# VectorE alone drains the units made ahead; the first negated copies come later in ScalarE's order; a fifth seven-product pair in layer 0's key and query units

## The chip, the cores and the metric

The kernel runs on one core of one Trainium2 chip. The metric is the device time of one launch in microseconds (us), with all weights read from HBM. A run is the median of several executions; one execution is recorded by the hardware profiler, and the views quoted below are of that one.

## The reference

Two layers of a hybrid decoder trunk on x of 256 rows by 2048 columns, all float32. The part that matters here is matrix products of 256 rows with weights that are read once:

```python
def hybrid_layer(x, attn_norm, w_in, ...):
    h = rms_norm(x, attn_norm)
    proj = jnp.einsum('bsd,de->bse', h, w_in)          # 2048 x 6160
    g_q, g_k, g_v, g_gate, g_lr, s_q, s_k, s_v = jnp.split(proj, COL_SPLITS, axis=-1)
    o_gla = gla_chunked(...)                           # gated linear attention, 8 heads
    o_sb = stick_breaking_attention(sq, sk, s_v)       # 8 heads
    mixed = jnp.concatenate([o_gla, o_sb], axis=-1)
    x = x + jnp.einsum('bse,ed->bsd', mixed, w_o)      # 2048 x 2048
    hm = rms_norm(x, mlp_norm)
    up = jnp.square(jax.nn.relu(jnp.einsum('bsd,df->bsf', hm, w_up)))   # 2048 x 8192
    return x + jnp.einsum('bsf,fd->bsd', up, w_down)   # 8192 x 2048

def reference(x, ...):
    for l in range(DEPTH):                             # DEPTH = 2
        x = hybrid_layer(x, ...)
    return x
```

## The kernel before

**Products.** A float32 product is made of three TensorE products in the rounded type fp32r: high part of the activation by `whi`, high by `wlo`, low by `whi` (`product`, L1231, L1234, L1235; the narrower projections of the attention stage do the same in L630 to L632). Each raw weight tile (1 MB, loaded by SP in L1023) is therefore made twice: ScalarE (ACT) rounds it to `whi` (L1098), then VectorE (DVE) makes `wlo` = raw - `whi` (L1102).

**Units and pairs.** Work goes in units of 1024 output columns by 2048 weight rows, eight pairs of 256 rows, numbered 0 to 7, in an order of steps given by a table. The kinds are g (gate), o (output projection, two units), up and down (16 units a layer), and iv, ik, iq: values, keys and queries made ahead for the next layer (for layer 0 they are the first big units of the program, in the text the first stage; for layer 1 they end layer 0's stage). A plain pair takes 24 products in two steps of 12 (banks 2 and 4, then 3 and 8). A seven-product pair takes 21 in four steps of 6, 6, 6 and 3 (banks 2 and 3, 5 and 7, 1 and 6, 4): it works like Winograd's scheme, and for it VectorE makes sums of weight tiles (`ts`, and two sums into the raw tile, L876) and both engines make other forms of the activation (L471, L488, L492). The tables EACH, FEWER, LATER, O0, O1 and those in OWN hold the order of steps, the seven-product pairs, and the pairs whose weights come by another way: for these GpSimd's queue (POOL) loads the rounded tile `chi` (L1059, function `high`), ScalarE writes `dlo` = -`chi` (L1063, `negated`), and a second DMA adds the weights into `dlo` (L1066). EACH is the order of all three units of the first stage; in layer 0, iv goes by FEWER, ik and iq by LATER.

**What sets the order.** TensorE, SP and POOL work in the order written. For ScalarE and VectorE a planner (`Plan`, `add(engine, cost, function, dependencies...)`) sorts the instructions by due times at build time; the engines then run strictly in that order. `held_tile` (L1054) is a tiny ScalarE write that gives the first three `chi` tiles a place; it is added with no dependency.

**Drains.** The eight accumulators m1 to m8 (bank 1 to 8) of a unit hold seven-product and plain sums and are put together in `up_tail`, which serves up units and the three kinds made ahead (`into` is False for these, and only their code changes). VectorE combines two tiles at a time (`combine`, L876 in the trace). In the kernel before, ScalarE copies bank 1 (L1366), VectorE forms w = b6 - b1, y10 = b5 + w, then w += b7 in place; banks 2 and 3 are added from the bank; banks 4 and 8 are copied by ScalarE first (L1391), and the second read of bank 5 waits for the copy of bank 8. After the last unit of a stage the banks are given back, and the first accumulator of the attention stage (`acc`, L630) lies on bank 5.

**Opening.** Before the first unit, TensorE makes a projection into `acc` (L630 to L632), whose two halves ScalarE copies out in L922 (`values`).

Of the kernel before, what the change touches and what calls it, by code (L numbers as in the profile page):

```python
# [11 lines left out]
F32R = mybir.dt.float32r  # L12
# [11 lines left out]
FEWER = [0, 0, 1, 2, 7, 4, 1, 1, 1, 6, 7, 6, 6, 6, 2, 3, 3, 3, 3, 5, 4, 5], (1, 3, 6), (2, 4)  # L24
# [3 lines left out]
O0 = [4, 5, 7, 4, 6, 6, 0, 0, 0, 7, 1, 0, 1, 1, 1, 5, 2, 2, 2, 2, 3, 3], (0, 1, 2), (5, 7)  # L28
O1 = [4, 6, 4, 1, 1, 2, 1, 5, 1, 2, 0, 0, 2, 2, 0, 5, 0, 3, 6, 3, 7, 7], (0, 1, 2), (5, 6)
SEEDED = (("down", 0), ("down", 1), ("o", 1))  # L30
SPARE = ("sxh",)
OWN = {
    ("up", 0): ([2, 5, 5, 5, 5, 1, 1, 1, 1, 2, 0, 0, 0, 3, 4, 0, 3, 3, 3, 6, 4, 6, 6, 6, 7, 7], (0, 1, 3, 5, 6), (2, 4)),
    ("up", 0, 0): ([0, 0, 3, 4, 3, 3, 1, 3, 4, 1, 1, 1, 5, 5, 2, 5, 5, 6, 6, 2, 6, 6, 7, 7], FAST, (2, 4)),
    ("up", 1): ([7, 7, 5, 5, 4, 5, 5, 1, 1, 1, 2, 3, 1, 3, 3, 3, 4, 6, 6, 6, 6, 0, 2, 0], FAST, (2, 4)),
    ("down", 0): ([0, 0, 1, 1, 1, 3, 4, 1, 3, 5, 3, 3, 4, 5, 5, 5, 2, 6, 6, 6, 6, 7, 7, 2], FAST, (2, 4)),
    ("down", 1): ([7, 7, 3, 3, 4, 3, 3, 5, 5, 5, 4, 5, 1, 1, 1, 1, 0, 0, 2, 0, 0, 6, 6, 6, 6, 2], (0, 1, 3, 5, 6), (2, 4)),
}
CAST, AHEAD_BY = 3, 1
FIRST_RAWS = 6  # L40
# [134 lines left out]
def trunk_kernel(  # L175
# [275 lines left out]
    def forms(op, i, t, tag):  # L451
# [21 lines left out]
        def high():  # L473
            if e:
                if both:
                    if tag in SPARE:
                        op.x[i] = act_tile(F32R, (P, 4, 2, P))
                    else:
                        op.x[i] = tmp(tag + "k", [P, 4, 2, P], F32R, bufs=1)
                elif keep:  # L480
                    op.x[i] = act_tile(F32R, (P, 4, 2, P))
                else:
                    op.x[i] = tmp(tag, [P, 3, 2, P], F32R, bufs=len(FAST))
# [375 lines left out]
    def ordered(l, units, hT, rst, ug, gates_t, mixed=None, ons=None):  # L859
# [182 lines left out]
        def rounded(u, j, s):  # L1042
# [314 lines left out]
        def up_tail(u):  # L1357
# [6 lines left out]
            def copy():  # L1364
                box[0], box[1] = act_tile(F32, (P, NT, 512)), act_tile(F32, (P, NT, 512))
                nc.scalar.activation(box[0][:, 0, :], banks[1], AF.Copy)  # L1366

            def new_dw():
# [12 lines left out]
            if not into:  # L1381
# [2 lines left out]
            def half(h, p):  # L1384
                box["r", h] = []
                for tt, m in enumerate(((2, 4), (3, 8))[h]):
                    before = p[m]
                    if tt:
                        free[m] = before = [add(
                            "ACT", A1,  # L1390
                            lambda m=m, h=h: nc.scalar.activation(  # L1391
# [7 lines left out]
                    users = box.setdefault("users", []) if tt else []  # L1399
                    a = vector(  # L1400
                        y(h, tt), y(h, tt), (lambda: box["w"]) if tt else bk(m), before,
                        box["s"][2 * h + tt], users, op=ALU.subtract if m == 4 else ALU.add,
                    )
                    a.give = len(users)
                    users.append(a)
                    if not tt:
                        free[m] = [a]

                    def relu(tt=tt):
# [556 lines left out]
```

## Time and profile before

| | us |
|---|---|
| median of 3 runs | 2145.78 |
| the runs | 2145.78, 2146.07, 2139.18 |
| profiled execution | 2145.65 |
| its span | 2144.0 |
| granted TensorE clock, mean of full | 0.996 |
| TensorE busy | 2117.9 |
| VectorE busy | 1936.9 |
| ScalarE busy | 1509.6 |
| GpSimd busy | 279.1 |

Times in views count from the start of the span. A timeline row reads: start, duration, engine, line, operation, output<-inputs, shape, count, and in brackets how long the engine had been idle before and what released it. In a row that stands for several instructions the duration is their sum, or for DMA issues the stretch over which they were issued. A row of a queue (SPq) is the issue of a transfer, not its landing. A matmul's duration covers its way through the array, so the pace is read from start to start.

### The profile page before, as it was taken

What the parts mean: (1) busy time and instruction counts of PE and PEld (TensorE: products, weight loads), DVE (VectorE), ACT (ScalarE), POOL (GpSimd) and SP (SyncE); (2) the same over time, 40 slices, a digit from 0 to 9 for tenths busy, and PEclk for the clock granted to TensorE, in tenths of its full rate; (3) what the DMA queues carried; (4) which work ended last, traced back from release to release, by engine and by line L of the source; (5) the groups of instructions that cost most, each with busy time, mean ns of one, the idle gap of its engine ahead of it and who ended that gap; (6) DMA issues with size and microseconds to landing.
All of it is one profiled execution on the core that took longest, in us unless ns stands there. A gap on an engine that the chain in (4) does not pass through costs nothing.

```text
span 2144.0 us, 28336 instructions
## 1 busy us (share of the span) xinstructions
PE 2117.9 (99%) x10040; PEld 1762.7 (82%) x10040; DVE 1936.9 (90%) x2658; ACT 1509.6 (70%) x2044; POOL 279.1 (13%) x394
## 2 busy tenths in 40 slices
PE   8999999999999999999999999999999999999998
PEld 6878888888888888888888888888888888888887
DVE  5887868999999999999998786699999999999998
ACT  6666667777677777668776575677776776786775
POOL 0110001111111111111111000011111111111110
PEclk9999999999999999999999999999999999999999
DMA  8765348788988988987988553678889888889886
GB/s 304 215 192 184 124 136 251 223 251 244 260 258 240 273 255 231 275 261 227 260 252 260 158 173 118 212 220 243 255 253 254 253 259 249 250 256 255 250 246 197
DMA packets 160691, 497.16 MB, mean 232 GB/s; under 512 B 10682, under 2 KB 19458, under 8 KB 160548
## 3 DMA queue, kind: packets, MB, share of 16 engines
q1 hardware_dynamic: 100900, 319.16, 41.3%
q0 software_dynamic: 59648, 176.18, 37.0%
q8 instruction: 79, 1.29, 0.2%
q14 instruction: 64, 0.52, 0.1%
HBM read 493.20 MB, written 2.10 MB: 231 GB/s over the span
## 4 chain that ended last, share of the span: by engine, by line
PE 91%; DVE 3%; ACT 3%; DMA 2%; issue 1%; POOL 0%; ACTq 0%; DVEq 0%
PE acc L630 3%; PE acc L632 3%; PE acc L631 3%; DMA raw<-in_w_in_dram 1%; DVE wlo L1102 1%; ACT whi L611 0%; DMA raw<-in_w_o_dram 0%; ACT whi L1098 0%; DMA chi<-in_w_in_dram 0%; PE ps L1903 0%; DVE wlo L613 0%; PE ps L1896 0%; DVE act L876 0%; PE ps L741 0%; PE ps L1853 0%
## 5 line engine op out<-in xcount | busy, mean ns | idle before, releaser
L1102 DVE TENSOR_TENSOR wlo<-raw,whi 128x1024 fp32r<-128x1024 f32 (+1 forms) x697 | 749.7, 1081 | 75.3 <-ACT whi L1098 41.2
L1098 ACT ACTIVATE whi<-raw 128x1024 fp32r<-128x1024 f32 (+1 forms) x697 | 648.9, 947 | 212.6 <-DVE raw L876 77.8
L1063 ACT ACTIVATE dlo<-chi 128x1024 fp32r<-128x1024 f32 x168 | 177.7, 1058 | 102.1 <-DMA chi<-in_w_in_dram 8.8
L1098 ACT ACTIVATE whi<-ts 128x1024 fp32r<-128x1024 f32 x177 | 187.3, 1058 | 70.0 <-DVE ts L876 33.9
L876 DVE TENSOR_TENSOR ts<-raw 128x1024 f32<-128x1024 f32 x177 | 215.5, 1218 | 11.3 <-DMA raw<-in_w_in_dram 8.6
L1102 DVE TENSOR_TENSOR wlo<-ts,whi 128x1024 fp32r<-128x1024 f32 x177 | 215.3, 1216 | 1.8 <-ACT whi L1098 1.7
L630 PE MATMUL acc<-whi,act 128*128 128x512 f32 (+2 forms) x384 | 142.4, 371 | 4.2 <-DVE act L876 4.2
L611 ACT ACTIVATE whi<-raw 128x1024 fp32r<-128x1024 f32 (+2 forms) x98 | 88.6, 908 | 69.7 <-PE acc L632 66.5
L632 PE MATMUL acc<-whi,act 128*128 128x512 f32 (+2 forms) x384 | 137.7, 359 | 0.0
L631 PE MATMUL acc<-wlo,act 128*128 128x512 f32 (+2 forms) x384 | 137.5, 358 | 0.0
L613 DVE TENSOR_TENSOR wlo<-raw,whi 128x1024 fp32r<-128x1024 f32 (+2 forms) x98 | 100.6, 1031 | 34.8 <-ACT whi L611 34.6
L876 DVE TENSOR_TENSOR raw<-raw 128x512 f32<-128x512 f32 x177 | 121.1, 684 | 1.8
L876 DVE TENSOR_TENSOR raw<-ts,raw 128x512 f32<-128x512 f32 x177 | 120.7, 682 | 0.1
L1059 POOL DMA_DIRECT2D chi<-in_w_up_dram x64 | 38.1, 595 | 515.0 <-PE m__2883_13592 L1235 34.8
L1059 POOL DMA_DIRECT2D chi<-in_w_down_dram x64 | 41.6, 650 | 424.6 <-PE m__914_4357 L1235 22.1
L630 PEld LDWEIGHTS acc<-whi,act 128*128 128x128 f32 x384 | 73.4, 191 | 17.1 <-DVE act L876 5.0
L1066 POOL DMA_DIRECT2D dlo<-in_w_down_dram x64 | 65.3, 1020 | 151.9 <-ACT dlo L1063 123.5
L632 PEld LDWEIGHTS acc<-whi,act 128*128 128x128 f32 x384 | 73.2, 191 | 10.4
L631 PEld LDWEIGHTS acc<-wlo,act 128*128 128x128 f32 x384 | 73.3, 191 | 8.9 <-DVE wlo L613 0.2
L1410 ACT ACTIVATE act<-act,st 128x512 f32<-128x512 f32 x88 | 62.3, 717 | 19.1 <-DVE act L876 18.6
L1066 POOL DMA_DIRECT2D dlo<-in_w_up_dram x64 | 57.9, 905 | 54.8 <-ACT dlo L1063 54.0
L492 DVE TENSOR_TENSOR act<-t,act 128x512 fp32r<-128x512 f32 x94 | 63.6, 682 | 0.0
(4536 smaller groups left out, 5809.3 us busy)
## 6 DMA issues: line engine op xcount, KB each, us to landing
raw<-in_w_up_dram SPq DMA_DIRECT2D x96, 1024.0 KB, 6.8
raw<-in_w_down_dram SPq DMA_DIRECT2D x96, 1024.0 KB, 8.3
raw<-in_w_in_dram SPq DMA_DIRECT2D x72, 1024.0 KB, 7.0
chi<-in_w_up_dram POOLq DMA_DIRECT2D x64, 512.0 KB, 5.2
dlo<-in_w_up_dram POOLq DMA_DIRECT2D x64, 512.0 KB, 7.7
chi<-in_w_down_dram POOLq DMA_DIRECT2D x64, 512.0 KB, 6.1
dlo<-in_w_down_dram POOLq DMA_DIRECT2D x64, 512.0 KB, 8.0
raw<-in_w_o_dram SPq DMA_DIRECT2D x24, 1024.0 KB, 7.7
```

The source lines that it names most:

```text
L492: nc.vector.tensor_tensor(d[:, :, 1, :], src, f32(d[:, :, 0, :]), ALU.subtract)
L611: newest["hi"] = nc.scalar.activation(h, r, AF.Copy).ins
L613: newest["lo"] = nc.vector.tensor_tensor(lo[:, q : q + step, :width], r, f32(h), ALU.subtract).ins
L630: nc.tensor.matmul(o, xh[:, sl], whi[:, j, :width], start=first, stop=False)
L631: nc.tensor.matmul(o, xh[:, sl], wlo[:, j, :width], start=False, stop=False)
L632: st["mm"] = nc.tensor.matmul(o, xl[:, sl], whi[:, j, :width], start=False, stop=last).ins
L876: nc.vector.tensor_tensor(dst, a, b, op)
L1059: nc.gpsimd.dma_start(flat("h"), src)
L1063: nc.scalar.activation(box["l"], f32(box["h"]), AF.Copy, scale=-1.0)
L1066: nc.gpsimd.dma_start(flat("l"), src, accum_op=ALU.add)
L1098: nc.scalar.activation(box["h"][:, :n], src(), AF.Copy)
L1102: nc.vector.tensor_tensor(box["l"][:, :n], src(), f32(box["h"][:, :n]), ALU.subtract)
```

## The change

Four things change. First, in `up_tail` for iv, ik and iq (six units in all) ScalarE's copies of banks 4 and 8 go; VectorE reads these banks itself, writes b7 + w straight into y01, gives w's tile back, and makes the second read of bank 5 at once from y01. Second, `held_tile` gets a dependency, `before[2]`, a product of the opening. Third, LATER and the operand hT (`FAST_OF["ht"]`) have pairs 0, 1, 3, 5 and 6 as seven-product pairs instead of 1, 3, 5 and 6. Fourth, the order of steps in all the tables is another. Of the tables EACH and LATER stand here; FEWER, O0, O1 and the five of OWN differ in their order alone (`bufs=4` is the value that it had).

```diff
-EACH = [0, 0, 1, 1, 1, 2, 7, 3, 3, 3, 3, 2, 5, 5, 5, 5, 4, 1, 6, 6, 6, 4, 6, 7], FAST, (2, 4)
+EACH = [7, 7, 1, 1, 0, 1, 2, 5, 2, 5, 5, 3, 5, 3, 3, 4, 6, 1, 6, 6, 6, 3, 4, 0], FAST, (2, 4)
-LATER = [0, 4, 0, 5, 5, 3, 5, 5, 4, 3, 3, 2, 1, 1, 3, 1, 1, 2, 6, 6, 6, 6, 7, 7], FAST, (2, 4)
+LATER = [2, 5, 5, 5, 5, 2, 6, 6, 6, 3, 6, 4, 3, 3, 3, 1, 1, 1, 4, 1, 0, 0, 0, 0, 7, 7], (0, 1, 3, 5, 6), (2, 4)
-FAST_OF = {"sxh": (0, 1, 3, 5, 6), "sx": (0, 1, 3, 5, 6)}
+FAST_OF = {"ht": (0, 1, 3, 5, 6), "sxh": (0, 1, 3, 5, 6), "sx": (0, 1, 3, 5, 6)}
...
-            if sums and i in (FAST if op is hT else FAST_OF["sxh"]):
+            if sums and i in FAST_OF["ht" if op is hT else "sxh"]:
...
-                first = add("ACT", 0.2, held_tile)
+                first = add("ACT", 0.2, held_tile, before[2])
...
-                a = vector(y(1, 0), bk(5), lambda: box["w"], w, p[5])
-                b = vector(lambda: box["w"], bk(7), lambda: box["w"], w, a, p[7])
+                a = vector(y(1, 0), bk(5), dw, w, p[5])
+                b = vector(dw if into else y(0, 1), bk(7), dw, w, a, p[7])
+                box["s"] = (w, b, a, b)
                 free.update({1: [c], 6: [w], 5: [a], 7: [b]})
-                box["s"] = (w, b, a, b)
+                if not into:
+                    b.give = 1
+                    box["s"] = (w, b, a, vector(y(1, 1), bk(5), y(0, 1), b, p[5]))
+                    free[5] = [a, box["s"][3]]
...
-                    before = p[m]
-                    if tt:
+                    before = [p[m], box["s"][3] if m == 4 and not into else []]
+                    if tt and into:
                         free[m] = before = [add("ACT", A1, ...
...
-                    if m == 8:
+                    if m == 8 and into:
...
+                    if tt and into:
+                        a = vector(y(h, 1), y(h, 1), dw, before, box["s"][2 * h + 1], users, op=minus)
...
+                    else:
+                        a = vector(
+                            y(h, tt), bk(m), y(h, tt), before, box["s"][2 * h + tt], op=minus
+                        )
                         free[m] = [a]
```

Over the whole program TensorE has 6 products fewer, VectorE 14 instructions more, ScalarE one fewer.

ScalarE at the opening, before the change (the three small writes are `held_tile`; `dlo` are the negated copies; `raw_396` is the first raw tile; `act_382<-acc_145` are the copies of L922):

```order
L1054 ACTIVATE chi_66_398<-act_43_304 128x1
L1054 ACTIVATE chi_67_400<-act_43_304 128x1
L1054 ACTIVATE chi_68_403<-act_43_304 128x1
L1063 ACTIVATE dlo_71_410<-chi_66_398 128x1024
L1063 ACTIVATE dlo_73_414<-chi_67_400 128x1024
L1098 ACTIVATE whi5_74_418<-raw_65_396 128x1024
L922 ACTIVATE act_55_382<-acc_13_145 128x512
L1098 ACTIVATE whi_79_431<-raw_65_396 128x1024
L922 ACTIVATE act_55_382<-acc_13_145 128x512
```

ScalarE at the same place after the change:

```order
L1054 ACTIVATE chi_68_402<-act_43_304 128x1
L1054 ACTIVATE chi_69_404<-act_43_304 128x1
L1054 ACTIVATE chi_70_407<-act_43_304 128x1
L1098 ACTIVATE whi5_72_412<-raw_65_396 128x1024
L922 ACTIVATE act_55_382<-acc_13_145 128x512
L1098 ACTIVATE whi_76_421<-raw_65_396 128x1024
L922 ACTIVATE act_55_382<-acc_13_145 128x512
L1098 ACTIVATE whi_88_443<-raw_66_398 128x1024
L488 ACTIVATE act_90_454<-t2_73_414 128x4x128
L1098 ACTIVATE whi_93_466<-ts_89_452 128x1024
L1063 ACTIVATE dlo_94_475<-chi_68_402 128x1024
```

The two negated copies moved from ahead of the first `whi` to places behind the fourth and the fifth `whi` of the new row; the first ends the piece above, the second follows one `whi` later. The small writes stay, and `chi` loads with them.

VectorE where the second unit of the first stage (ik) ends and the third (iq) begins, before the change (`act_218`, `act_219` are the two halves of ik's result, `t2_222` is w, `ts_220` is the first sum of iq's weights; `m5__172` is bank 5 and so on):

```order
L1102 TENSOR_TENSOR wlo_217_1082<-raw_170_859,whi5_213_1071 128x1024
L876 TENSOR_TENSOR ts_220_1093<-raw_202_1011 128x1024
L876 TENSOR_TENSOR t2_222_1103<-m6__177_879,act_218_1090 128x512
L1102 TENSOR_TENSOR wlo_224_1110<-raw_170_859,whi_215_1078 128x1024
L876 TENSOR_TENSOR act_218_1090<-act_218_1090,m2__158_802 128x512
L876 TENSOR_TENSOR act_219_1091<-m5__172_863,t2_222_1103 128x512
L1102 TENSOR_TENSOR wlo_227_1129<-raw_202_1011,whi_221_1098 128x1024
L876 TENSOR_TENSOR act_219_1091<-act_219_1091,m3__165_830 128x512
L876 TENSOR_TENSOR raw_202_1011<-ts_220_1093,raw_202_1011 128x512
L1102 TENSOR_TENSOR wlo_231_1152<-ts_220_1093,whi_228_1137 128x1024
L876 TENSOR_TENSOR act_219_1091<-m5__172_863,act_219_1091 128x512
```

The same place after the change (`act_216`, `act_215` are the halves, `ts_226` is iq's first sum):

```order
L876 TENSOR_TENSOR t2_220_1091<-m6__180_893,act_215_1076 128x512
L1102 TENSOR_TENSOR wlo_221_1096<-raw_169_852,whi_219_1086 128x1024
L876 TENSOR_TENSOR act_216_1077<-m5__171_856,t2_220_1091 128x512
L876 TENSOR_TENSOR act_215_1076<-m2__157_797,act_215_1076 128x512
L876 TENSOR_TENSOR act_215_1076<-m7__172_860,t2_220_1091 128x512
L876 TENSOR_TENSOR ts_226_1124<-raw_203_1021 128x1024
L876 TENSOR_TENSOR act_216_1077<-m5__171_856,act_215_1076 128x512
L876 TENSOR_TENSOR act_216_1077<-m3__162_820,act_216_1077 128x512
L876 TENSOR_TENSOR act_215_1076<-m4__160_810,act_215_1076 128x512
L876 TENSOR_TENSOR act_216_1077<-m8__165_831,act_216_1077 128x512
L1102 TENSOR_TENSOR wlo_231_1158<-raw_203_1021,whi_222_1101 128x1024
```

The drains of banks 5, 2 and 7 moved ahead of iq's first weight sum, the second read of bank 5 comes before those of banks 3, 4 and 8, and banks 4 and 8 are now inputs of VectorE.

VectorE at the end of layer 0's stage, where attention of layer 1 follows, before the change (`m5__2278` is bank 5, L613 is the `wlo` of the attention stage's products):

```order
L876 TENSOR_TENSOR act_2314_10907<-act_2314_10907,t2_2316_10913 128x512
L876 TENSOR_TENSOR act_2315_10908<-act_2315_10908,m3__2269_10677 128x512
L291 CAST ident16_2327_11002<-ident_83 128x128
L306 CAST tri_2329_11004<-t2_2333_11013 128x128
L308 CAST nones_2330_11005<-t2_2334_11014 128x128
L411 TENSOR_SCALAR st_2343_11053<-st_2337_11028 128x8
L613 TENSOR_TENSOR wlo_2349_11067<-raw_2339_11032,whi_2348_11066 128x2x272
L876 TENSOR_TENSOR act_2315_10908<-m5__2278_10722,act_2315_10908 128x512
L418 TENSOR_TENSOR st_2345_11055<-st_2344_11054 128x8
L876 TENSOR_TENSOR act_2315_10908<-act_2315_10908,t2_2316_10913 128x512
```

The same place after the change:

```order
L876 TENSOR_TENSOR act_2328_10925<-m5__2278_10687,t2_2329_10930 128x512
L876 TENSOR_TENSOR act_2327_10924<-m7__2280_10694,t2_2329_10930 128x512
L876 TENSOR_TENSOR act_2327_10924<-m2__2269_10650,act_2327_10924 128x512
L876 TENSOR_TENSOR act_2328_10925<-m5__2278_10687,act_2327_10924 128x512
L613 TENSOR_TENSOR wlo_2339_11002<-raw_2335_10983,whi_2338_11001 128x2x272
L876 TENSOR_TENSOR act_2327_10924<-m4__2271_10662,act_2327_10924 128x512
L876 TENSOR_TENSOR act_2328_10925<-m3__2276_10681,act_2328_10925 128x512
L291 CAST ident16_2340_11017<-ident_83 128x128
L306 CAST tri_2342_11019<-t2_2346_11028 128x128
L876 TENSOR_TENSOR act_2328_10925<-m8__2289_10730,act_2328_10925 128x512
```

The second read of bank 5 moved from the end of the drains to a place ahead of those of banks 4, 3 and 8.

More of the change, by code (lines that the diff above doesn't have):

```diff
@@ L22 @@
 FAST = (1, 3, 5, 6)
[L23 to L26 removed]
+EACH = [7, 7, 1, 1, 0, 1, 2, 5, 2, 5, 5, 3, 5, 3, 3, 4, 6, 1, 6, 6, 6, 3, 4, 0], FAST, (2, 4)
+FEWER = [0, 0, 3, 4, 2, 7, 3, 3, 3, 6, 7, 6, 2, 6, 6, 1, 1, 1, 1, 4, 5, 5], (1, 3, 6), (2, 4)
+LATER = [2, 5, 5, 5, 5, 2, 6, 6, 6, 3, 6, 4, 3, 3, 3, 1, 1, 1, 4, 1, 0, 0, 0, 0, 7, 7], (0, 1, 3, 5, 6), (2, 4)
+FAST_OF = {"ht": (0, 1, 3, 5, 6), "sxh": (0, 1, 3, 5, 6), "sx": (0, 1, 3, 5, 6)}
 TWO_WAYS = (("sxh", 0), ("sx", 0))
[L28 to L29 removed]
+O0 = [6, 7, 6, 4, 5, 4, 0, 0, 1, 0, 5, 0, 1, 2, 2, 7, 1, 1, 2, 2, 3, 3], (0, 1, 2), (5, 7)
+O1 = [5, 7, 7, 2, 2, 2, 2, 0, 6, 0, 0, 0, 1, 1, 1, 1, 5, 6, 3, 3, 4, 4], (0, 1, 2), (5, 6)
 SEEDED = (("down", 0), ("down", 1), ("o", 1))
@@ L32 @@
 OWN = {
[L33 to L37, printed above, removed]
+    ("up", 0): ([4, 1, 1, 1, 1, 6, 6, 6, 6, 2, 3, 3, 3, 5, 2, 3, 5, 5, 5, 0, 4, 0, 0, 0, 7, 7], (0, 1, 3, 5, 6), (2, 4)),
+    ("up", 0, 0): ([0, 0, 4, 3, 3, 1, 3, 1, 4, 3, 5, 1, 5, 1, 2, 5, 5, 6, 2, 6, 6, 6, 7, 7], FAST, (2, 4)),
+    ("up", 1): ([7, 7, 5, 5, 2, 5, 5, 3, 3, 3, 6, 3, 4, 6, 6, 6, 2, 1, 1, 1, 1, 0, 0, 4], FAST, (2, 4)),
+    ("down", 0): ([0, 0, 1, 1, 3, 2, 1, 1, 3, 4, 5, 3, 3, 5, 5, 5, 2, 6, 6, 6, 6, 7, 4, 7], FAST, (2, 4)),
+    ("down", 1): ([7, 7, 6, 6, 4, 6, 6, 1, 1, 1, 4, 1, 5, 5, 5, 5, 0, 0, 2, 0, 0, 3, 3, 3, 3, 2], (0, 1, 3, 5, 6), (2, 4)),
 }
@@ L482, in high @@
                 else:
-                    op.x[i] = tmp(tag, [P, 3, 2, P], F32R, bufs=len(FAST))
+                    op.x[i] = tmp(tag, [P, 3, 2, P], F32R, bufs=4)
                 todo.append((op.x[i], e[0]))
@@ L1366, in copy, with dw @@
                 nc.scalar.activation(box[0][:, 0, :], banks[1], AF.Copy)
+            def dw():
+                return box["w"]
             def new_dw():
@@ L1395, in half @@
                         )]
-                    if m == 8:
+                    if m == 8 and into:
                         before = vector(y(1, 1), bk(5), y(1, 1), before, p[5])
                         free[5] = free[5] + [before]
[L1399 to L1406, printed above, removed]
+                    users = box.setdefault("users", []) if tt and into else []
+                    minus = ALU.subtract if m == 4 else ALU.add
+                    if tt and into:
+                        a = vector(y(h, 1), y(h, 1), dw, before, box["s"][2 * h + 1], users, op=minus)
+                        a.give = len(users)
+                        users.append(a)
+                    else:
+                        a = vector(
+                            y(h, tt), bk(m), y(h, tt), before, box["s"][2 * h + tt], op=minus
+                        )
                         free[m] = [a]
```

## The prediction

> **What bounds the kernel now.** I read the page's totals first, then TensorE's waits, then the busy time by stage. Every sum below is against the profiled execution: 2145.65 us, a span of 2144.0; the median of the runs, 2145.78, stands beside it within 0.2 us.
>
> ```profile
> PE 2117.9 (99%) x10040; PEld 1762.7 (82%) x10040; DVE 1936.9 (90%) x2658; ACT 1509.6 (70%) x2044; POOL 279.1 (13%) x394
> ...
> PE m__86_446 L1231 <- ACT whi L1098: 8.1, 1, 8.1
> PE m__230_1143 L1231 <- DVE act L876: 4.2, 1, 4.2
> PE acc L630 <- DVE act L876: 4.2, 2, 2.7
> ...
> PE m__694_3310 L1231 <- DVE act L1517: 0.3, 1, 0.3
> ...
> 360.00:1140.00 780.00, 780.00 (x3537) 647.20 (x3537) 751.67 (x988) 575.29 (x754) 115.48 (x148) 1.00 0.87 252
> 1126.00:1207.00 81.00, 81.00 (x359) 67.10 (x358) 69.98 (x80) 51.76 (x63) 9.06 (x15) 1.00 0.78 231
> 1380.00:2120.00 740.00, 740.00 (x3348) 613.70 (x3347) 710.78 (x930) 543.23 (x698) 108.56 (x139) 1.00 0.87 253
> ```
>
> The first row gives each engine's busy us. A wait row gives who waited for whom: us in total, times, longest. A stretch row reads: length, then busy us of TensorE, its weight loads, VectorE, ScalarE and GpSimd, TensorE's clock, the share of the DMA engines. In the long middle of both layers TensorE never stops at full clock: nothing can be gained there but by fewer products, while VectorE has only 28.3 us to spare in 780. TensorE loses time at four places: the three waits named (one stands for two places). All four are places that this diff touches, so I price it place by place.
>
> **The opening.** Two products of one bank and weight tile, 47.98 and 50.74 below, are 12 apart: 0.23 us a product.
>
> ```profile
> 17.73 28.54 SPq L1023 DMA_DIRECT2D raw<-in_w_in_dram  x6
> ...
> raw<-in_w_in_dram SPq DMA_DIRECT2D x2, 1024.0 KB, 11.7
> ...
> 29.82 0.48 ACT L1054 ACTIVATE chi<-act 128x1 fp32r<-128x1 f32 x3
> 30.43 1.80 POOL L1059 DMA_DIRECT2D chi<-in_w_in_dram  x3 [29.04 <-ACT chi L1054]
> 33.68 0.39 PE L632 MATMUL acc<-whi,act 128*128 128x512 f32 x1
> 37.76 1.06 ACT L1063 ACTIVATE dlo<-chi 128x1024 fp32r<-128x1024 f32 x1 [7.46 <-DMA chi<-in_w_in_dram]
> 39.12 0.89 POOL L1066 DMA_DIRECT2D dlo<-in_w_in_dram  x1 [6.89 <-ACT dlo L1063]
> ...
> dlo<-in_w_in_dram POOLq DMA_DIRECT2D x1, 512.0 KB, 6.0
> ...
> 41.10 1.04 ACT L1098 ACTIVATE whi<-raw 128x1024 fp32r<-128x1024 f32 x1
> 42.20 0.79 PE L1231 MATMUL m__86_446<-whi,act 128*128 128x512 f32 x1 [8.13 <-ACT whi L1098]
> 47.98 0.39 PE L1231 MATMUL m__88_448<-whi,act 128*128 128x512 f32 x1
> 50.74 0.39 PE L1231 MATMUL m__86_446<-whi,act 128*128 128x512 f32 x1
> ...
> 40.00:50.00 10.00, 7.34 (x21) 5.52 (x22) 7.82 (x11) 8.45 (x10) 0.89 (x2) 0.62 0.92 199
> ...
> L1102 DVE TENSOR_TENSOR wlo<-raw,whi 128x1024 fp32r<-128x1024 f32 x520 | 632.5, 1217 | 68.8 <-ACT whi L1098 39.9 <-ACT dlo L1063 13.3 <-issue 2.9
> ```
>
> SP issues six raw loads from 17.73 on; the first two take 11.7 to land (second row), the first by 29.4. Yet ScalarE copies the first `whi` only at 41.10: ahead of it stand two `negated` copies, and the first waits 7.46 us for a chi transfer that no early product needs. From 33.68 to 47.98 TensorE starts 13 products: 13 x 0.23 = 2.99 of 14.30 us, so 11.3 are lost (8.13 of waiting, the rest a clock of 0.62 and a wait for `wlo`).
>
> With the copies behind the fourth and the fifth `whi`, the first `whi` runs right behind the chi tiles, 30.3 to 31.4, and its `wlo` (1.22) ends by 32.6, ahead of the last product of `acc` at 33.68 + 0.23 = 33.9: no wait, no slow clock. New waits: ScalarE now stands in order at L922, which can't copy `acc` before 33.9; then 0.58 for it, 1.04 for the second `whi`, 1.22 for its `wlo`: 36.8, where TensorE is after 12 products, at 36.7. A wait of 0.1 to 0.2 there, and two like it up to the next pair: I take 0.7. So -10.6. SP's raw loads are issued as before; on POOL the chi loads keep their place, the `dlo` accumulates behind them go out later. Those hide behind the first steps: pair 2 comes seventh, after 54 products, at 33.9 + 54 x 0.23 + 0.7 = 47.0. By the order its `negated` copy ends at about 40.2; issue (0.89) and the 6.0 us from issue to landing that the accumulate issued at 39.12 took give 47.1. That is no reserve: each us that it lands later is paid. I put 1 us into the costs below for it, with ends 0 and 4 (a landing like the opening's raw loads, 11.7 in place of 6, less what TensorE's queue absorbs).
>
> **The third unit of the first stage (iq).**
>
> ```profile
> 113.42 14.76 DMA raw<-in_w_in_dram
> ...
> 120.00:130.00 10.00, 7.43 (x32) 5.51 (x30) 2.55 (x4) 2.96 (x4) 0.56 (x1) 1.00 1.05 348
> ...
> 127.31 0.39 PE L1235 MATMUL m__167_840<-whi,act 128*128 128x512 f32 x1
> 128.20 1.23 DVE L876 TENSOR_TENSOR ts<-raw 128x1024 f32<-128x1024 f32 x1 [7.45 <-DMA raw<-in_w_in_dram]
> 131.08 0.68 DVE L876 TENSOR_TENSOR act<-act,m__158_802 128x512 f32<-128x512 f32 x1
> 131.90 0.47 PE L1231 MATMUL m__230_1143<-whi,act 128*128 128x512 f32 x1 [4.21 <-DVE act L876]
> 136.32 0.39 PE L1231 MATMUL m__235_1168<-whi,act 128*128 128x512 f32 x1
> ```
>
> VectorE stands 7.45 us at a weight sum (`ts`) whose raw tile is late: 14.76 us, the DMA engines full. The drain of bank 2 stands behind it in VectorE's order, and TensorE waits 4.21 for that bank, then runs slow: 13 products in 9.01 us instead of 2.99, 6.0 lost. After the change the drains of banks 6, 5, 2 and 7 stand ahead of that `ts`, and pair 1's raw tile is the third load of its group instead of the fourth, with the loads around it further apart. At 348 GB/s one load of 1 MB is 3.0 us of all engines, so it lands 3 us sooner for the place alone. I take -5.5: 0.5 us stays for the drains of banks 4 and 8, now VectorE's too. If the raw tile is as late as before, the products of pair 1 wait in bank 2's stead and 6.0 stays lost; both ends go into the range.
>
> **The two ends, where attention follows.**
>
> ```profile
> 174.18 0.39 PE L1235 MATMUL m__238_1179<-whi,act 128*128 128x512 f32 x1
> 174.68 0.58 ACT L1391 ACTIVATE act<-m__238_1179 128x512 f32<-128x512 f32 x1
> 175.29 0.69 DVE L876 TENSOR_TENSOR act<-m__242_1201,act 128x512 f32<-128x512 f32 x1
> 176.04 0.39 PE L630 MATMUL acc<-whi,act 128*128 128x272 f32 x1 [1.47 <-DVE act L876]
> 179.94 0.29 PE L630 MATMUL acc<-whi,act 128*128 128x272 f32 x1
> ...
> 1207.69 0.39 PE L1235 MATMUL m__2271_10683<-whi,act 128*128 128x512 f32 x1
> 1210.02 0.69 DVE L876 TENSOR_TENSOR act<-m__2278_10722,act 128x512 f32<-128x512 f32 x1
> 1210.77 0.39 PE L630 MATMUL acc<-whi,act 128*128 128x272 f32 x1 [2.69 <-DVE act L876]
> 1215.04 0.29 PE L630 MATMUL acc<-whi,act 128*128 128x272 f32 x1
> ```
>
> The first `acc` lies on bank 5, and its second read stands behind ScalarE's copy of bank 8. Losses between products: 1.86 - 0.23 = 1.6 and 3.08 - 0.23 = 2.85. From 176.04 to 179.94 are 30 narrow products, 0.13 each; from 1210.77 to 1215.04 are 21, so 4.27 - 2.73 = 1.5 more. Now the second read comes straight after bank 7's, before the last products: -1.6 and -4.4. Later waits (drains of banks 4 and 8 before the banks come round again) have the attention stage's slack.
>
> The slow stretch after 1210.77 followed a gap of 2.69 us. The Trainium skill, "TensorE: Matmul & The Clock Gate", section "What's actually happening", gives the slow clock only after an idle window of about 3.4 us; by it the sum would be 1.5 us less. The row is against it: products at 1210.77 to 1215.04 ran at half speed.
>
> **What costs.**
>
> ```profile
> L876 DVE TENSOR_TENSOR ts<-raw 128x1024 f32<-128x1024 f32 x177 | 215.5, 1218 | 11.3 <-DMA raw<-in_w_in_dram 8.6 <-DMA raw<-in_w_down_dram 1.4 <-DMA raw<-in_w_o_dram 0.2
> L876 DVE TENSOR_TENSOR act<-act,t 128x512 f32<-128x512 f32 x52 | 35.2, 683 | 2.2 <-ACT t L1478 1.6 <-ACT act L1391 0.6
> ```
>
> An add from a bank (0.68 and 0.69 above) costs what one from SBUF does (683 ns): eight adds a unit before and after, so VectorE gains no work; ScalarE loses 12 copies of 0.58, hidden anyway. The fifth pair in ik and iq of layer 0 takes 6 products away, 6 x 0.23 = -1.4, and adds on VectorE a `ts` (1.22), two sums of 128x512 (0.68, as the adds) and a longer `wlo` and forms, near 4.5 us a unit: 9 us against the 11.0 to spare in 1126:1207. Hidden, but only just; without that cover up to 9 us. The drains of banks 4 and 8 now stand in VectorE's queue behind one add and often a `wlo` (0.68 + 1.22): 0 to 1.9 us at each of four boundaries; most of it falls before TensorE comes back to the bank. With the `dlo` and O0's later read of bank 7 I take +2.0 in all, ends 0 and 12. The new orders of the 32 up and down units and 4 output units move no work; in the middle they can only cost. I take nothing: VectorE has 28.3 / 19 = 1.5 us a unit (a unit is 177 to 180 products, 41 us) to absorb what they shift.
>
> Sum: -10.6 - 5.5 - 1.6 - 4.4 - 1.4 + 2.0 = -21.5: 2145.65 - 21.5 = 2124.2, and I say 2124.
>
> **Rivals.**
> - Half of it: the `dlo` or the raw tile of iq lands late after all (the DMA engines are at 0.92 and 1.05 there), or what TensorE wins at an end is waited away in the attention stage. Losing one of 6.0 (iq, or both ends together) or 4 plus a slow clock's 3 (`dlo`) leaves 14 to 15: 2131; losing two, 2137. For it: both places wait on transfers near the limit. Against: the drains no longer queue behind a `ts`.
> - No change: the fifth pair eats its 11 us of cover and the orders cost 0.3 us a unit (36 x 0.3 = 11): 2140 to 2146. The diff does do what it says: the order of ScalarE's instructions at the opening is changed as told.
> - Slower: the new tables. One wait of VectorE's lag in each of the 32 up and down units, at a boundary where a bank is drained behind a weight sum, as in the row at 131.90. It cancels the gain at 21.5 / 32 = 0.67 us a unit and is told as slower beyond 0.87; at 1.2 (one `ts`) it gives 2124 + 38 = 2162. For it: VectorE is busy 751.67 of 780. Against: the same load of work, and in those units the list of waits names none of TensorE as long as the 0.3 us of m__694, which is in the output projection.
>
> **How the numbers follow.** About 0.3% (6.4 us) is what the measurement can tell. The forecast, 2117 to 2131: 0.72 (its lower end is all four places at their full 24.9, no cost, and a run as far under the median as the third was in part). Half of it, 2131 to 2139: 0.15. No change: 0.08. Slower: 0.05. The range 2117 to 2137 leaves some 0.16 out above and 0.03 below. Faster 0.87, same 0.08, slower 0.05.
>
> **What would show it.** Right: ScalarE's first `whi` at about 30.4, TensorE without a gap at 33.9, the step of pair 2 within 1 us of 47; no TensorE wait above 1 us at iq; the first `acc` product 0.23 us behind the last of iq at both ends at full clock; the middle busy throughout. Wrong: a wait of `m` banks on VectorE's L876 or L1102 that recurs by unit; a wait for `dlo` near 47; VectorE full in the last 80 us before layer 1's attention.

## The result, and the profile after

| | before | changed |
|---|---|---|
| median of the runs, us | 2144.51 | 2125.11 |
| the runs | 2145.78, 2146.07, 2139.18, 2143.23 | 2126.9, 2124.66, 2125.08, 2125.15 |
| profiled execution | 2145.65 | 2126.9 |
| its span | 2144.0 | 2125.0 |

The ratio is 0.9915, with an interval of 0.9897 to 0.9934: faster, by 18 us by the ratio and 19.4 between the medians. The forecast was 2124 (2117 to 2137).

Totals of the changed kernel, busy us by engine, from the page (ScalarE has 2038 instructions after 2044, six fewer and not one as told above); under them TensorE's waits, each with us in total, times, and longest:

```profile
PE 2110.3 (99%) x10034; PEld 1754.8 (83%) x10034; DVE 1944.8 (92%) x2672; ACT 1503.8 (71%) x2038; POOL 285.5 (13%) x394
```

```profile
PE m__2791_13130 L1234 <- DMA dlo<-in_w_o_dram: 1.3, 1, 1.3
...
PE m__3603_16913 L1438 <- DVE act L876: 0.9, 1, 0.9
PE acc L630 <- ACT whi L611: 0.8, 1, 0.8
PE m__83_436 L1234 <- DVE wlo L1102: 0.8, 1, 0.8
PE m__695_3307 L1231 <- DVE act L1526: 0.8, 1, 0.8
PE m__1081_5127 L1231 <- ACT m__1081_5127 L1293: 0.7, 1, 0.7
```

The three waits of 8.1, 4.2 and 4.2 us are gone. What stands at the top now are single waits of about 1 us, most of them new. (The changed source is nine lines longer from `up_tail` on: its L1526 is L1517 of the kernel before, where 0.3 us was lost.) The stretches show that the middle of both layers is no longer quite full; in the same columns as in the prediction:

```profile
340.00:1120.00 780.00, 779.11 (x3529) 645.45 (x3528) 751.51 (x991) 572.89 (x755) 118.09 (x149) 1.00 0.86 251
1110.00:1190.00 80.00, 80.00 (x355) 66.24 (x354) 76.83 (x92) 54.49 (x64) 12.89 (x23) 1.00 0.79 217
1360.00:2100.00 740.00, 737.38 (x3332) 610.34 (x3331) 707.79 (x921) 537.58 (x695) 109.43 (x138) 1.00 0.86 252
```

The opening, from the timeline of the changed kernel:

```profile
29.38 1.15 ACT L1098 ACTIVATE whi<-raw 128x1024 fp32r<-128x1024 f32 x1
32.95 0.39 PE L632 MATMUL acc<-whi,act 128*128 128x512 f32 x1
33.17 0.39 PE L1231 MATMUL m__83_436<-whi,act 128*128 128x512 f32 x1
35.89 0.39 PE L1231 MATMUL m__85_438<-whi,act 128*128 128x512 f32 x1
38.57 1.04 ACT L1063 ACTIVATE dlo<-chi 128x1024 fp32r<-128x1024 f32 x1
39.92 0.89 POOL L1066 DMA_DIRECT2D dlo<-in_w_in_dram  x1 [8.40 <-ACT dlo L1063]
43.04 0.50 PE L1234 MATMUL m__83_436<-wlo,act 128*128 128x512 f32 x1 [0.77 <-DVE wlo L1102]
47.05 0.39 PE L1231 MATMUL m__83_436<-chi,act 128*128 128x512 f32 x1
47.28 0.39 PE L1234 MATMUL m__83_436<-dlo,act 128*128 128x512 f32 x1
```

The first `whi` runs at 29.38 instead of 41.10. TensorE goes from the projection into the first unit without a gap: 13 products take 35.89 - 32.95 = 2.94 us instead of 14.30. The `dlo` of pair 2 is there in time: TensorE takes it at 47.28, straight behind the product before.

The start of iq, where the second of the old waits was, and the two ends, from the timeline of the changed kernel:

```profile
113.12 0.68 DVE L876 TENSOR_TENSOR act<-m__157_797,act 128x512 f32<-128x512 f32 x1
114.31 1.22 DVE L876 TENSOR_TENSOR ts<-raw 128x1024 f32<-128x1024 f32 x1
116.19 0.39 PE L1235 MATMUL m__165_831<-whi,act 128*128 128x512 f32 x1
116.41 0.39 PE L1231 MATMUL m__229_1140<-whi,act 128*128 128x512 f32 x1
...
156.99 0.39 PE L1235 MATMUL m__236_1175<-whi,act 128*128 128x512 f32 x1
157.21 0.28 PE L630 MATMUL acc<-whi,act 128*128 128x272 f32 x1
...
1189.68 0.39 PE L1235 MATMUL m__2289_10730<-whi,act 128*128 128x512 f32 x1
1189.90 0.28 PE L630 MATMUL acc<-whi,act 128*128 128x272 f32 x1
```

Bank 2 is drained at 113.12, ahead of the weight sum, which itself no longer waits; iq follows ik by 0.22 us. At both ends the first narrow product follows the last wide one by 0.22 us.

For the accounts below each trace is cut at three marks: the last L632 product of the opening's projection, the first narrow L630 product of each attention stage, and the last product of the program. "First" is the stretch up to the first attention, "layer 0" from there to the second, "layer 1" from there to the end.

| us | first | layer 0 | layer 1 |
|---|---|---|---|
| before (33.68, 176.04, 1210.77, 2138.11) | 142.36 | 1034.73 | 927.34 |
| changed (32.95, 157.21, 1189.90, 2119.14) | 124.26 | 1032.69 | 929.24 |
| difference | -18.10 | -2.04 | +1.90 |

With the marks' own start (-0.73; this projection ended between 32.95 and 34.22 in the traces taken) this is the 19.0 us of the spans.

### The profile page after: what moved, and what is told of

Read it like the earlier page. It is cut to its first block, busy times and chain, and to the rows that moved or that the text cites. A ratio compares the mean times of both kernels' runs of the same rounds, so it can differ in the third digit from the quotient of the medians.

```text
span 2125.0 us, 28371 instructions
## 1 busy us (share of the span) xinstructions
PE 2110.3 (99%) x10034; PEld 1754.8 (83%) x10034; DVE 1944.8 (92%) x2672; ACT 1503.8 (71%) x2038; POOL 285.5 (13%) x394
## 4 chain that ended last, share of the span: by engine, by line
PE 86%; issue 5%; DMA 3%; DVE 3%; ACT 2%; POOL 1%; POOLq 0%; DVEq 0%; ACTq 0%
PE acc L630 3%; PE acc L632 3%; PE acc L631 3%; DMA raw<-in_w_down_dram 1%; DVE wlo L1102 1%; DMA raw<-in_w_in_dram 1%; DMA raw<-in_w_up_dram 1%; DMA dlo<-in_w_o_dram 1%; DMA raw<-in_w_o_dram 0%; ACT whi L611 0%; DVE wlo L613 0%; PE ps L1912 0%; ACT whi L1098 0%; POOL dlo L1066 0%; PE ps L741 0%
## 5 line engine op out<-in xcount | busy, mean ns | idle before, releaser
L630 PE MATMUL acc<-whi,act 128*128 128x512 f32 (+2 forms) x384 | 141.0, 367 | 0.8 <-ACT whi L611 0.8
L632 PE MATMUL acc<-whi,act 128*128 128x512 f32 (+2 forms) x384 | 136.8, 356 | 0.0
L613 DVE TENSOR_TENSOR wlo<-raw,whi 128x1024 fp32r<-128x1024 f32 (+2 forms) x98 | 100.3, 1031 | 28.0 <-ACT whi L611 27.9
L630 PEld LDWEIGHTS acc<-whi,act 128*128 128x128 f32 x384 | 72.3, 188 | 13.2 <-issue 3.4
L632 PEld LDWEIGHTS acc<-whi,act 128*128 128x128 f32 x384 | 72.3, 188 | 10.4
L1066 POOL DMA_DIRECT2D dlo<-in_w_down_dram x64 | 59.7, 933 | 114.0 <-ACT dlo L1063 101.8
L1066 POOL DMA_DIRECT2D dlo<-in_w_up_dram x64 | 64.1, 1001 | 71.7 <-ACT dlo L1063 68.5
```

What stands on the lines that cost most here:

```text
L613: newest["lo"] = nc.vector.tensor_tensor(lo[:, q : q + step, :width], r, f32(h), ALU.subtract).ins
L630: nc.tensor.matmul(o, xh[:, sl], whi[:, j, :width], start=first, stop=False)
L632: st["mm"] = nc.tensor.matmul(o, xl[:, sl], whi[:, j, :width], start=False, stop=last).ins
L1066: nc.gpsimd.dma_start(flat("l"), src, accum_op=ALU.add)
```

## The experiments

The twelve runs came in three groups; each was timed beside runs of the kernel before on its own chip. Their medians, and the stretches of their traces:

| run | median | before beside it | first | layer 0 | layer 1 |
|---|---|---|---|---|---|
| e1, held_tile alone | 2128.94 | 2143.81 | 127.57 | 1034.97 | 928.30 |
| e2, drains alone | 2136.21 | 2143.81 | 135.38 | 1032.23 | 926.23 |
| e3, EACH alone | 2137.78 | 2143.81 | 135.05 | 1034.46 | 927.23 |
| e4, change, old O0, O1, OWN | 2121.66 | 2143.81 | 125.18 | 1031.56 | 925.85 |
| e5, change without held_tile | 2135.93 | 2145.43 | 134.46 | 1033.11 | 927.22 |
| e6, change without drains | 2131.53 | 2145.43 | 125.29 | 1034.69 | 929.08 |
| e7, before, less VectorE work | 2139.81 | 2145.43 | 135.93 | 1034.78 | 928.38 |
| e8, held_tile and drains | 2126.20 | 2145.43 | 127.11 | 1032.68 | 925.72 |
| e9, change again | 2124.63 | 2143.70 | 124.06 | 1033.50 | 927.41 |
| e10, change, old O0, O1 | 2125.91 | 2143.70 | 123.40 | 1032.34 | 925.92 |
| e11, change, old OWN | 2124.81 | 2143.70 | 124.30 | 1031.33 | 927.92 |
| e12, change, four pairs | 2125.94 | 2143.70 | 124.56 | 1032.74 | 925.88 |

**e1: held_tile alone.**

```diff
-                first = add("ACT", 0.2, held_tile)
+                first = add("ACT", 0.2, held_tile, before[2])
```

> The kernel before with one line changed: held_tile gets the dependency before[2]. Theory (order of ScalarE): this alone frees the opening, since the two negated copies move behind the fourth whi; the first whi runs within 1 us of the raw tile, TensorE goes on without a gap after the projection, and of the 11.3 us lost there some 10 come back: 2134 to 2136. The 6.0 us at the start of iq and the losses at the two ends (1.6 and 4.4) stay. Rival (the step order of EACH is needed too): with pair 2 sixth in the old EACH, 42 products after the projection, its dlo lands late, TensorE waits 2 to 4 us for it in a slow clock: gain 5 to 8, 2138 to 2141.

2128.94; ratio 0.9928 (0.9903 to 0.9953). Neither theory: 15 us instead of 10 or less. Its waits of TensorE:

```profile
PE acc L630 <- DVE act L876: 4.2, 2, 2.7
...
PE m__83_436 L1234 <- DMA dlo<-in_w_in_dram: 0.9, 1, 0.9
PE m__81_434 L1234 <- DVE wlo L1102: 0.8, 1, 0.8
```

The ends' 4.2 stand as before. The wait at the opening is gone, at the price of 0.9 for the `dlo` and 0.8 for a `wlo`. But the 4.2 at iq is gone as well, though neither the order of VectorE there nor the order of loads was touched: the weight sum (113.23) still stands ahead of the drain of bank 2 (116.11).

**e2: the drains alone** (`up_tail` of the changed kernel in the kernel before).

```diff
+                if not into:
+                    b.give = 1
+                    box["s"] = (w, b, a, vector(y(1, 1), bk(5), y(0, 1), b, p[5]))
...
-                    if m == 8:
+                    if m == 8 and into:
```

> The kernel before with the drains of up_tail alone changed. Theory: both ends gain (1.6 and 4.4, since bank 5 is read before the last products), 2139 to 2141; the opening keeps its 11.3 us. At iq the weight sum still stands ahead of the drain of bank 2 in VectorE's order, and the raw tile is as late: the 6.0 us stay. Rival (the drains through ScalarE caused the wait at iq): the 4.2 us wait at iq goes too, 2134 to 2136.

2136.21; ratio 0.9970 (0.9956 to 0.9984), between the two, nearer to the rival. The profiled execution gives the parts:

```profile
PE m__86_446 L1231 <- ACT whi L1098: 7.8, 1, 7.8
...
PE m__232_1155 L1231 <- DVE act L876: 1.3, 1, 1.3
```

The opening keeps its wait, the ends lost theirs, and at iq 4.2 us became 1.3, at another bank. The weight sum stood ahead of bank 2's drain in VectorE's order here too. So that order alone was not what made the wait long.

**e3: the order EACH alone.**

```diff
-EACH = [0, 0, 1, 1, 1, 2, 7, ...
+EACH = [7, 7, 1, 1, 0, 1, 2, ...
```

> The kernel before with the new order of steps in EACH alone (the first stage's three units). Theory: the opening keeps its 11.3 us (the negated copies still stand ahead of the first whi), the ends keep theirs; at iq the raw tile comes earlier and the drain of bank 2 stands ahead of the weight sum, so most of the 6.0 us goes: 2139.5 to 2141. Rival (the drains by VectorE are what frees iq): the order alone leaves the wait, 2144 to 2146.

2137.78; ratio 0.9974 (0.9964 to 0.9984): the theory, a little better.

```profile
PE m__86_446 L1231 <- ACT whi L1098: 8.2, 1, 8.2
PE acc L630 <- DVE act L876: 4.1, 2, 2.7
```

Opening and ends as before, iq free. So each of the three edits by itself frees iq, or nearly: they share a cause that the prediction hadn't named.

**e7: less work for VectorE in ik.** The kernel before; the fourth weight sum of the seven-product pairs is left out in that one unit, so its result is no longer the reference's. The planner also moved a few weight instructions within ik; VectorE's order where iq begins is that of the kernel before.

```diff
-            t4 = vector(w(1, 0), w(0, 1), w(1, 0), t2, low[1:3])
-            readers.extend((t13, t2, t4))
+            if l < 0 and u == 1:
+                t4 = t2
+                readers.extend((t13, t2))
+            else:
+                t4 = vector(w(1, 0), w(0, 1), w(1, 0), t2, low[1:3])
+                readers.extend((t13, t2, t4))
```

> The kernel before, in whose second unit (ik of the first stage) the fourth weight sum (the one into the raw tile, 128x512, for four pairs) is left out: 2.7 us less work on VectorE, nothing else moved at iq. Theory (VectorE lags in ik, so it gives a raw slot back late and the loads bunch): the load for iq's first sum lands 3 us or more sooner, the 4.2 us wait for bank 2 falls under 1.5 us: 2138 to 2141. Rival (the loads are late by the DMA engines' limit alone): the wait stays above 3 us: 2143 to 2146.

2139.81; ratio 0.9978 (0.9969 to 0.9988): the theory, and the wait at iq is not short but absent. The stretch from 100 to 112 us, first of the kernel before, then of this one (after the length stand the busy us of TensorE, of its weight loads, and of VectorE):

```profile
100.00:112.00 12.00, 12.00 (x54) 9.80 (x53) 12.00 (x15) 9.39 (x12) 1.57 (x3) 1.00 0.81 209
```

```profile
100.00:112.00 12.00, 12.00 (x54) 9.94 (x54) 10.56 (x13) 8.43 (x10) 2.26 (x3) 1.00 0.78 190
```

In the kernel before, VectorE has not a moment of idle time there; TensorE still runs, on what was made ahead. The last weight sum of ik (in e7 also iq's first) from the timeline, and under it the load for iq's first sum from the list of DMA issues (the last number is us to landing), in the kernel before, in this one, and in e1:

```profile
110.37 1.21 DVE L876 TENSOR_TENSOR ts<-raw 128x1024 f32<-128x1024 f32 x1
```

```profile
raw<-in_w_in_dram SPq DMA_DIRECT2D x1, 1024.0 KB, 14.8
```

```profile
106.25 1.22 DVE L876 TENSOR_TENSOR ts<-raw 128x1024 f32<-128x1024 f32 x1
...
123.90 1.23 DVE L876 TENSOR_TENSOR ts<-raw 128x1024 f32<-128x1024 f32 x1 [2.65 <-DMA raw<-in_w_in_dram]
```

```profile
raw<-in_w_in_dram SPq DMA_DIRECT2D x1, 1024.0 KB, 12.6
```

```profile
98.32 1.22 DVE L876 TENSOR_TENSOR ts<-raw 128x1024 f32<-128x1024 f32 x1
```

```profile
raw<-in_w_in_dram SPq DMA_DIRECT2D x1, 1024.0 KB, 10.9
```

What the load itself waited for stands in the trace as well. First the list of waits of SP's queue in the kernel before, from 105 to 122 us, then the chain of work that led to the late load (start, duration, what):

```profile
SPq L1023 <- DVE wlo L1102: 34.2, 5, 21.8
```

```profile
112.79 0.61 DVE wlo L1102
113.40 0.02 issue
113.42 14.76 DMA raw<-in_w_in_dram
```

The load goes out 0.02 us after a `wlo` of VectorE ends; by the list such a `wlo` is what the queue waited for, and by the code it is a reader of the tile whose slot the load takes. In e7, e1, e2 and e3 the list of SP's queue names nothing but that `wlo` for L1023 either.

iq's first product could start at 127.31 + 0.23 = 127.54 in the kernel before, and starts at 127.61 in e7 and 118.57 in e1. Against that the last weight sum of ik comes 17.2 us ahead in the kernel before, 21.4 in e7, 20.3 in e1, and by the same reckoning 20.1 in e2 (106.70, 126.75) and 19.1 in e3 (106.87, 125.97). The load for iq's sum is issued 14.1 us ahead in the kernel before (at 113.42, 1.2 behind another load, with two more 4.7 and 6.0 behind it) and takes 14.8; in e7, e2 and e1 it is issued 16.4, 16.5 and 16.2 ahead and takes 12.6, 11.5 and 10.9. So VectorE is behind in ik, the load goes out 2 us late, and it lands some 4 us late; the weight sum waits for it, and the drain of bank 2 stands behind the weight sum, w and a `wlo`. Every edit that gets VectorE 2 to 4 us ahead in ik breaks this early. That less work for VectorE in ik is enough is shown by e7, and that the load waited for VectorE by the chain above. Why the late load also took longer is not: it went out closer to its neighbours, but no run moved those alone. In e3 other orders, of the loads and of the drain of bank 2, are at work too. That VectorE was behind because it had stood idle at the opening (its first `wlo` came at 42.18) fits e1, where only the opening was changed (31.03 there), and was not tried by itself.

**e5 and e6: the change without one of its two code edits.** e5 takes `before[2]` out again, e6 has the old `up_tail`.

```diff
-                first = add("ACT", 0.2, held_tile, before[2])
+                first = add("ACT", 0.2, held_tile)
```

> The changed kernel without the dependency of held_tile: the two negated copies stand ahead of the first whi again. Theory: the 8 us wait and the slow clock behind it come back, 11.3 less the new waits of the freed opening (about 2): 2133 to 2136; the start of iq stays free, since the new EACH and the new drains are there. Rival (the opening alone freed iq, as the run of that one line suggests, which gained 15 instead of 10): iq's wait comes back too, 2139 to 2141.

2135.93; ratio 0.9956 (0.9942 to 0.9971): the theory. The wait at the first product is back, and there is none at iq:

```profile
PE m__86_446 L1231 <- ACT whi L1098: 8.1, 1, 8.1
```

One wait of 1.4 us at L1526 in layer 1 is the longest of its kind in any run.

```diff
-                    if m == 8 and into:
+                    if m == 8:
...
```

> The changed kernel with the drains of before in up_tail (ScalarE copies banks 4 and 8). Theory: the two ends lose again, 1.6 and 4.4, iq stays free by its order and the early opening: 2130 to 2132. Rival (VectorE's queue at the banks 4 and 8 costs elsewhere): less than 4 us longer than the change, 2126 to 2129.

2131.53; ratio 0.9934 (0.9920 to 0.9949): the theory. The ends are back, iq is free:

```profile
PE acc L630 <- DVE act L876: 4.7, 2, 3.2
```

**e4: the change with the old orders of the middle** (O0, O1, OWN).

```diff
-O0 = [6, 7, 6, 4, 5, 4, ...
+O0 = [4, 5, 7, 4, 6, 6, ...
...
-    ("up", 0): ([4, 1, 1, 1, 1, 6, ...
+    ("up", 0): ([2, 5, 5, 5, 5, 1, ...
```

> The changed kernel with the tables O0, O1 and OWN of before (EACH, FEWER and LATER stay new). Theory: the new tables of the output projection and of the up and down units only cost, some 3 to 4 us in new waits (1.7 at a dlo of the output projection of layer 1, 1.2 at a seed of the first down unit, about 1 at L1526, about 1.2 at L1438), so the time falls to 2121 to 2123. Rival: the new tables fit the new start of layer 0's stage and take away other waits; without them the time is the same or up to 3 us longer, 2125 to 2128.

2121.66; ratio 0.9897 (0.9875 to 0.9918): as the theory had it, 3.5 us under the changed kernel's 2125.11, and the lowest time measured. The two were timed on different occasions and their intervals overlap, so "faster than the change" is not shown; e10 and e11 below, each with a part of these old orders, don't show it either.

**e8: the two code edits alone**, all tables as before, four pairs.

```diff
+                first = add("ACT", 0.2, held_tile, before[2])
...
+                    box["s"] = (w, b, a, vector(y(1, 1), bk(5), y(0, 1), b, p[5]))
```

> The kernel before with held_tile's dependency and the new drains, all tables as before, four seven-product pairs in ik and iq of layer 0. Theory: these two code edits give all of the gain that counts, opening and iq 15 and both ends 6, so 2122 to 2125, no slower than the whole change; the new tables and the fifth pair give less than they cost. Rival (the new tables are needed for the edits to work together): 2127 to 2131.

2126.20; ratio 0.9910 (0.9895 to 0.9924). Between theory and rival, and not to be told from the whole change: two edits of the code carry the gain. What EACH still adds is in the first stretch, 127.11 against 124.26: e8 has a `dlo` wait of 1.0 there, as e1 had, and one of 0.8 at iq. In these two traces the layers give it back, 1958.40 in sum against 1961.93.

**e9 to e12: which of the new tables costs.** Four kernels on one chip.

```diff
-O0 = [6, 7, 6, 4, 5, 4, ...      # e10: O0 and O1 of before
-    ("up", 0): ([4, 1, 1, ...      # e11: the five of OWN of before
-LATER = [2, 5, 5, 5, ...          # e12: LATER of before, "ht": FAST
```

> The changed kernel itself once more, as the measure for the three runs beside it: 2124 to 2127. If the new waits in the middle (1.7 at a dlo of the output projection, 1.4 at a seed of the first down unit, 1.6 at L1438) are the tables', the same ones recur within 0.5 us each; if they are chance of one execution, they change place.

> The changed kernel with O0 and O1 of before, the orders of the two output projection units of each layer. Theory: they hold some 2 of the 3.5 us that all old tables gave back, by the dlo wait of layer 1 (1.7) and the wait at L1526 (1.0 in layer 0): 1.5 to 2.5 us below the changed kernel beside it. Rival (the up and down orders hold it): less than 1 us below.

> The changed kernel with the five orders of OWN of before, those of the up and down units. Theory: the waits at a seed (1.4) and at L1438 (1.6) go, the dlo wait stays: 1 to 2.5 us below the changed kernel beside it. Rival (all of it was the output projection's orders): within 0.7 us of it.

> The changed kernel with LATER and hT's pairs of before: four seven-product pairs in ik and iq of layer 0 instead of five. Theory (VectorE has room for the fifth pair): six products more, 1 to 1.5 us longer than the changed kernel beside it, none of it in a wait. Rival (VectorE is too full at the end of layer 0's stage, so that the fifth pair costs what it gives): within 0.5 us or shorter.

2124.63 for the change; 2125.91 (e10), 2124.81 (e11), 2125.94 (e12); ratios 0.9913, 0.9912, 0.9913, 0.9919, each with some 0.0016 to both sides. As times e10 and e11 miss: they were to be 1 to 2.5 us lower and are 1.3 and 0.2 higher, which fits the rival of each, and those lay the cost to the other table; e12 is 1.3 higher, as expected of six products more, but within the spread. Single executions of e10 lie between 2121.83 and 2127.17, so an effect of 2 us is not to be had this way. The waits tell more. In the change again:

```profile
PE m__695_3307 L1231 <- DVE act L1526: 0.7, 1, 0.7
PE m__1081_5127 L1231 <- ACT m__1081_5127 L1293: 0.7, 1, 0.7
PE m__3144_14775 L1231 <- ACT m__3144_14775 L1293: 0.7, 1, 0.7
```

In e11, with the old orders of up and down:

```profile
PE m__2791_13130 L1234 <- DMA dlo<-in_w_o_dram: 1.1, 1, 1.1
PE m__695_3307 L1231 <- DVE act L1526: 0.9, 1, 0.9
```

The wait at L1526 (VectorE's read of a bank in layer 0's output projection) is 0.7 to 0.9 us in all six kernels with the new O0: the change, e5, e9, e11, e12, and e6, whose shorter source has that line as L1517. With the old O0 the same line costs less: 0.3 in the kernel before, 0.6 in e1, 0.4 in e7, 0.2 in e2, e4 and e8, and it is not in the lists of e3 and e10. So the new O0 makes a wait longer that was there, by 0.1 to 0.9 us. The seed at L1293 (ScalarE writes a bank before the first down unit) waits 0.6 to 0.7 in layer 0 of the change, e5, e9 and e10, and not in e11 and e4, but also not in e6 and e12, which have the new OWN; e7, with all the old tables, has 0.3 and 0.2 there in layer 1. So the longer ones were seen with the new OWN only, and it doesn't suffice. The `dlo` wait of layer 1's output projection comes in the change, in e6 and in e11 and not in e5, e9 or e12, which have the same O1: since the change has it (1.3) and e9, the same kernel, has not, it is chance of the execution. So is the 0.9 at L1438: it is not in e9, and e8, with the old tables, has one as long at another place. Of the waits that e9 was to repeat two came back and two did not. No combination was run that beats e4.

## Why the prediction was right

**The opening, -10.6.** Right in mechanism and size. The 11.3 us came back whole (2.94 for 14.30). The new waits were put at 0.7; the products of pair 2 start at 47.05, after 54 products from 33.17, which makes 47.05 - 33.17 - 54 x 0.227 = 1.6. So -9.7 by the trace. The largest, 0.77 at 43.04, is the `wlo` of pair 0, which was among the "two like it" put at 0.1 to 0.2. The `dlo` came in time, and the margin was wider than told: issued at 39.92 and 6.2 us under way it landed at 46.1, 1.2 ahead of its first product. The prediction added the 0.89 of the issue to a time that runs from the start of the issue, as the chain in e1 shows:

```profile
40.40 6.13 DMA dlo<-in_w_in_dram
46.54 0.04 issue
46.58 0.50 PE m__83_436 L1234
```

Some 0.9 of the 1.2 came from the new waits, which hold pair 2 back. In e1 and e8, where the old EACH has its pair 2 earlier, the `dlo` cost 0.9 and 1.0.

**The start of iq, -5.5.** The size was right (all 6.0 went), the reason was not the one that mattered, and that the size came out so is luck: each of three edits frees iq by itself, or nearly. The prediction laid the gain to the drains that moved ahead of the weight sum and to pair 1's place among the loads. e1 changed neither and freed iq all the same; e2 has the sum ahead of the drain still and keeps 1.3 of the 4.2 of waiting. The cause lay some 20 us earlier, in VectorE's lag in ik, which e7 shows: 2.7 us less work for it there and the wait was gone. The step that failed is the reading of the chain of waits, which ended at the late transfer of 14.76 us: that the DMA engines were full was seen, why the load went out only at 113.42, 1.2 us behind another, was not asked. It also means that this term was not the drains' to give. Taken alone the three edits bring 15, 8 and 6 us between the medians, 29 in all, and each of these holds most or all of iq's 6, which can be won but once.

**The two ends, -1.6 and -4.4.** Right: 1.86 and 3.08 between products became 0.22 and 0.22, and the 21 narrow products that ran slow run at full pace. e2, with the drains alone, has 0.22 and 0.23 there, and e6, the change without them, 1.84 and 3.62. As a time e6 is 6.4 us longer than the change (2131.53 against 2125.11), with 6.0 told; the two were timed on different occasions, and the ratios, each to the kernel before beside it, make it 4.

The slow stretch is the other 1.5 us of this term. The Trainium skill, "TensorE: Matmul & The Clock Gate", section "What's actually happening", has the slow clock come after an idle window of about 3.4 us. The traces are against it once more. In e1 the same gap of 2.69 us is followed by narrow products 0.23 apart, from 1196.36 to 1202.02, longer than in the kernel before; in the change, without a gap, the same 21 steps take 1192.54 - 1189.90 = 2.64 instead of 4.27.

**Fewer products, -1.4.** Not shown as a time. In e12 they are back and the median is 1.3 longer, not beyond the spread; its trace has layer 0 in 1032.74, against 1032.69 and 1033.50 in the two traces of the change, which have the wait at the seed besides. VectorE at the end of layer 0's stage went from 69.98 of 81 to 76.83 of 80 us, and TensorE is busy for all of the 80: the work of the fifth pair does fit, with 3.2 us to spare.

**Costs, +2.0 in all.** This is the term that was too small. Layer 0 should have gained 2.85 + 1.4 and gained 2.04, layer 1 should have gained 1.5 and lost 1.90: 2.2 and 3.4, in the change again 3.0 and 1.6. With 0.9 more at the opening the costs were some 5.5 to 6.5, within the ends of 0 and 12. "The new orders ... I take nothing" is the part that failed: the new O0 makes the wait at L1526 longer, the one at L1293 was seen with the new orders, and the middle is not busy throughout, but the waits are one here and there and not one in each unit as the slower rival had it. How much of the costs is the orders' stays open. By the same reckoning the layers cost 1.1 in e4 and 0.7 in e8, which have the old orders in the middle, against 5.6 and 4.6 in the two traces of the change; but in e12, with the new ones, only 0.9.

In the sum 21.5 was told; the medians differ by 19.4. That the median lies within 1.1 us of the forecast is in part luck: the profiled execution took 2126.9, 2.7 more than told, and 0.73 of its gain is only that the opening's projection ended earlier in it.

## What to carry to other kernels

An engine that works strictly in order turns one early instruction with a slow input into a stall for everything behind it: look at the first place where the engine that sets the time stands still and ask what heads the queue of the engine it waits for, not what that engine is busy with. Where a wait ends in a late transfer, go on back: ask when it was issued, what freed its slot, and whether the engine that freed it was running without a pause. And gains of edits that meet at one wait don't add up; run each of them alone before crediting the wait to one.

## What was not expected of the hardware

A 1 MB load took 7.0 us from issue to landing at 61 us of the kernel before and 14.8 at 113.42, with three other loads issued between 1.2 us ahead of it and 6.0 behind. In e7, e2 and e1 the load for the same tile had its neighbour 1.4, 1.7 and 2.2 us ahead instead of 1.2, and the next one 6.8 behind instead of 4.7, and it took 12.6, 11.5 and 10.9. So shifts of 1 to 3 us among neighbours went with up to 4 us of a load's time; GpSimd's transfers of 512 KB shifted as well, so that it is not shown which neighbour counts.

A pause of 2.69 us was followed by a slow stretch in all four traces that have it (the kernel before, e1, e3 and e7), and none followed the pauses of 1.45 to 1.47 us at the other end of the same four. The stretch was not always the same: narrow products were 0.23 apart for some 3.4 us in the kernel before and for 5.7 in e1.
